# RWKV-7 layer of a hybrid trunk: triangular 32x32 blocks inverted by doubling on TensorE instead of a lane solve on VectorE

## The chip, the cores and the metric

The program runs on one core of a Trainium2 chip. The metric is the device time of one execution in microseconds (us); a comparison rests on the median of several. Engines are named as the profile names them: PE is TensorE's matmul stream, PEld its weight loads, DVE is VectorE, ACT is ScalarE, POOL is GpSimd, SP is the engine that issues the DMAs. Each engine takes its own instructions in a fixed order and waits at the first one whose inputs are not there.

## The reference, cut to what matters

The network has four layers over 256 context tokens and 1024 image tokens, width 1024: layers 0 and 3 are gated linear recurrences, layer 1 is an mLSTM, layer 2 is RWKV-7 with 16 heads of 64, run forwards and backwards. The change is in layer 2 alone, whose recurrence is

```
def step(s, inp):
    r_t, w_t, kk_t, a_t, k_t, v_t = inp
    s = (s * w_t[..., None, :]
         - jnp.einsum('bhvk,bhk->bhv', s, kk_t)[..., None] * (kk_t * a_t)[..., None, :]
         + v_t[..., :, None] * k_t[..., None, :])
    return s, jnp.einsum('bhvk,bhk->bhv', s, r_t)
```

All of it is in float32. The kernel works on chunks of 64 tokens. Within a chunk the rank-one corrections form a unit lower triangular 64x64 system, so each chunk of each head and direction needs the inverse of one such matrix.

## The kernel before, in words

Layer 2 is the function `rwkv_scan`. It first builds constants and projects the first token block, and then runs one loop of 41 rounds over 40 batches. A batch is one pair of heads, both directions, and one block of 256 tokens of each direction, which is four chunks per direction, so 2 heads x 2 directions x 4 chunks = 16 triangular matrices. Four things make up a round n, written in this order: the chunk steps `chain` of batches n-1 and n (four calls; the state goes from one step to the next), `finish` of batch n-2, `inverse` of batch n+1, and `prep` of batch n+2. Beside these each round pulls a portion of "fill": the projections of the other token blocks (products with 128x128 weights into the PSUM pool `pz`, lines 110 to 112 and 899 to 901), the gate and the output projection. The fill of a round may not be issued before the last DVE instruction of an earlier round. A scheduler then sets the final order on each engine from this code; it may put an instruction of one batch between those of another.

`prep` (lines 991 to 1111) makes, among other things, the tile DG: the two 32x32 diagonal blocks of each matrix. The 128 partitions are 4 groups of 32 rows (2 heads x 2 diagonal blocks), and u = 0 to 7 runs over direction and chunk. The 32x32 block below the diagonal goes to the tile OF.

`inverse` (lines 1113 to 1182) has three parts. The lane solve: DVE transposes DG (line 1122, on a tile of 1024 columns of which a quarter is used), so that each lane holds a whole 32x32 matrix in its row (tile LN); then 14 steps of forward substitution on the two 16x16 diagonal blocks of each, two DVE instructions a step (lines 1139 and 1140); then DVE transposes back (line 1142, tile DF). One doubling from 16 to 32: POOL masks DG to the 16x16 block below the diagonal (tile DO), DVE masks and adds the identity (D16) and transposes it (E16, line 1146); PE multiplies 32 blocks of 32x32 (line 1152), ACT copies the result out of PSUM (QQ, line 1154), PE multiplies again (line 1157), DVE adds (line 1159) and transposes (line 1160). The last doubling, from 32 to 64, uses OF, 16 products twice (lines 1164 and 1170) and ACT copies into the tile DT, which `chain` reads at line 1215. The products of one doubling use one PSUM tile of the pool `pi`, which has one buffer and is also used by `kk_norm` in the fill (lines 957 and 965).

The constants `m16`, `off16` and `id32` are built before the loop by POOL selects through the helper `sel` (line 787).

Of the kernel before, what the change touches and what calls it, by code (L numbers as in the profile page):

```python
# [28 lines left out]
class Net:  # L29
# [731 lines left out]
    def rwkv_scan(self, es, hd, zd, yd, xd):  # L761
        nc = self.nc
        gate = self.mod["gate"]
        V, G, S = nc.vector, nc.gpsimd, nc.scalar
        mm = nc.tensor.matmul
        rp = es.enter_context(self.pool("rp", 2))
        one = es.enter_context(self.pool("r1", 1))
        psp = lambda n, b: es.enter_context(self.tc.tile_pool(name=n, bufs=b, space=PSUM))
        pz, px, pc, pi = psp("pz", 2), psp("px", 2), psp("pc", 3), psp("pi", 1)
        tile_ = lambda name, shape, dt=F32, bufs=2: rp.tile(shape, dt, tag=name, name=name, bufs=bufs)  # L770
# [10 lines left out]
        def cst(name, shape, fill=0.0):  # L781
            t = one.tile(shape, F32, name=name)
            G.memset(t, fill)
            return t

        def sel(t, pattern, base, cm, op=ALU.is_ge, fill=0.0):
            G.affine_select(out=t, in_=t, pattern=pattern, compare_op=op, fill=fill, base=base, channel_multiplier=cm)
# [14 lines left out]
                        in1=hm.unsqueeze(1).to_broadcast([128, 8, 2]), op=ALU.mult)  # L802
# [188 lines left out]
        def prep(n):  # L991
# [10 lines left out]
                V.tensor_copy(out=w2[d][r], in_=raw2[r])  # L1002
                self.lo(G, w2[d][hr[1 - d]], raw2[r], w2[d][r])
            lw = L[i]
            DG = DGs[n % len(DGs)]
            b["DG"], b["OF"] = DG, tile_("OF", [128, 8, 32])
            ts, ops = [], []
            for d in (0, 1):
                blk = order[d][i]
# [103 lines left out]
        def inverse(n):  # L1113

            i, e = batch(n)
            b = B[n]
            DG, OF, DT = b["DG"], b["OF"], DTs[n % 2]
            u8 = lambda t: t.unsqueeze(1).to_broadcast([128, 8, 32])
            l8 = lambda name, tag=None: rp.tile([128, 8, 32], F32, tag=tag or name, name=name, bufs=1)
            DO = l8("DO")  # L1120
            LN = tile_("LN", [128, 32, 32], bufs=1)
            V.transpose(out=LN, in_=DG.rearrange("p u t -> p t u"))
            self.tt(G, DO, DG[:, 0:8, :], u8(off16))
            full = LN.rearrange("p t s -> p (t s)")

            def ap(t0, tn, s0, sn, tb, sb):

                v = full[:, t0 * 32 + s0:t0 * 32 + s0 + 1]
                dims = [list(v.ap[0]), [16 * 33, 2], [0 if tb else 32, tn], [0 if sb else 1, sn]]
                return bass.AP(v.tensor, v.offset, dims)  # L1130

            for j in range(1, 15):
                n1 = 15 - j
                tmp = tile_("ltmp", [128, 2, 56], bufs=1)
                c = ap(j + 1, n1, j, j, False, True)
                x = ap(j, n1, 0, j, True, False)
                o = ap(j + 1, n1, 0, j, False, False)
                tv = tmp[:, :, 0:n1 * j].rearrange("p q (t s) -> p q t s", s=j)
                V.tensor_tensor(out=tv, in0=c, in1=x, op=ALU.mult)
                V.tensor_tensor(out=o, in0=tv, in1=o, op=ALU.add)  # L1140
            DF = tile_("DF", [128, 32, 32], bufs=1)
            V.transpose(out=DF.rearrange("p u t -> p t u"), in_=LN)
            D16, E16 = l8("D16"), l8("E16", "E")
            self.tt(V, D16, DF[:, 0:8, :], u8(m16))
            self.tt(V, D16, D16, u8(id32), ALU.add)
            V.transpose(out=E16, in_=D16)
            p8 = lambda: pi.tile([128, 8, 64], F32, tag="pi", name="pi")
            ps = p8()
            g4 = [slice(32 * g, 32 * g + 32) for g in range(4)]
            for u in range(8):  # L1150
                for g in g4:
                    mm(ps[g, u, 0:32], DO[g, u, :], E16[g, u, :], start=True, stop=True)
            QQ = l8("QQ", "Q8")
            S.copy(out=QQ, in_=ps[:, :, 0:32])
            for u in range(8):
                for g in g4:
                    mm(ps[g, u, 32:64], QQ[g, u, :], D16[g, u, :], start=True, stop=True)
            D32, E32 = l8("D32"), l8("E32", "E")
            V.tensor_tensor(out=D32, in0=D16, in1=ps[:, :, 32:64], op=ALU.add)
            V.transpose(out=E32, in_=D32)  # L1160
            ps = p8()
            for u in range(8):
                for hh in (0, 2):
# [120 lines left out]
                    return  # L1284

        early = True
        h0 = [tile_(t, [128, 4, 256], bufs=1) for t in ("LN", "DF")]
        for k in range(8):
            nc.sync.dma_start(out=h0[k // 4][:, k % 4, :], in_=hd[k][:, 0:256])
        for _ in group((0,), (4, 5, 1, 0, 2)):  # L1290
# [9 lines left out]
        for r in hr:  # L1300
# [3 lines left out]
            sel(mk[1][r, 0:64], [[1, 64]], -64, 1)  # L1304
            sel(mk[1][r, 64:128], [[-1, 64]], 0, 1)
            sel(mb[1][r], [[-1, 64]], 63, -1)
        m16, off16, id32 = cst("m16", [128, 32], 1.0), cst("off16", [128, 32], 1.0), cst("id32", [128, 32], 0.0)
        for g in range(4):
            r = slice(32 * g, 32 * g + 32)
            V.tensor_copy(out=id32[r], in_=self.ident[r, r])  # L1310
            sel(m16[r], [[1, 32]], -1, -1)

            sel(off16[r, :], [[0, 32]], 15, -1)
        V.memset(off16[:, 0:16], 0.0)
        V.tensor_tensor(out=m16, in0=m16, in1=off16, op=ALU.subtract)
        scm = []
        for d in (0, 1):
            t = cst(f"scm{d}", [128, 4, 65], 1.0)
            V.memset(t[:, :, 64 - 64 * d:65 - 64 * d], 0.0)
            scm.append(t)  # L1320
        sgs = [cst(f"sg{d}", [128, 4, 65]) for d in (0, 1)]
        DGs = [cst(f"DG{i}", [128, 32, 32]) for i in range(1)]
        DTs = [cst(f"DT{i}", [128, 8, 64]) for i in range(2)]
        st = [[one.tile([128, 64], F32, name=f"st{e}{d}") for d in (0, 1)] for e in range(4)]
        G0, G1, G2 = (0,), (1, 4), (2, 3)
# [157 lines left out]
```

## Time and profile before

| | |
|---|---|
| median of 3 runs (lowest, highest) | 4810.22 us (4805.49, 4817.24) |
| the profiled execution's own time | 4812.02 us |
| its span in the trace | 4810.3 us |
| mean granted TensorE clock in it | 0.849 of full speed |
| busy share of the span: PE, PEld, DVE, ACT, POOL | 85%, 69%, 73%, 44%, 48% |

The loop over the 40 batches lies between about 2080 and 4180 us. "Busy" is the time in which at least one instruction of an engine runs; PE's instructions overlap, and their ends are modelled by the profiler. The granted clock of a stretch is the mean of two levels, 1.2 and 2.4 GHz; 0.75 means that half of the stretch ran at each.

### The profile page before, as it was taken

To read this page: it belongs to the slowest core of one execution; us is meant where nothing else is said; L and a number is where in the kernel's file an instruction comes from. 1 tells how busy PE (TensorE), PEld (TensorE's weight loads), DVE (VectorE), ACT (ScalarE), POOL (GpSimd) and SP (SyncE) were. 2 spreads that over 40 slices of the span, in tenths; PEclk is the share of its full clock that TensorE was granted. 3 is DMA by queue.
4 is the path that set the end of the run, shared out by engine and by line. 5 is a ranking of instruction groups with operands and counts; after the bars stand their busy time and mean duration, and the time that the engine had idled before them with its cause. 6 is when DMAs were issued, how large, how long until landed. Compare 5 with 4: busy or idle time off the path is not lost. (4 is left out here: it accounts for less than half of the span.)

```text
span 4810.3 us, 84381 instructions
## 1 busy us (share of the span) xinstructions
PE 4103.1 (85%) x31940; PEld 3342.1 (69%) x31940; DVE 3495.0 (73%) x6520; ACT 2101.5 (44%) x4458; POOL 2304.7 (48%) x1995
## 2 busy tenths in 40 slices
PE   5887898999999989668888888779788897669988
PEld 5676686888888878545667666566666676557766
DVE  6988846555555542696888879988898899657884
ACT  3555513222222210555656545445555444247661
POOL 4566623333333331375556545445456554247662
PEclk9898898999999989768788867567688787679999
DMA  4222331222222242434444433223334453231123
GB/s 158 85 73 76 139 107 47 90 88 90 97 91 90 88 156 66 151 119 130 131 133 140 126 98 114 83 83 105 91 123 134 142 166 103 82 110 51 50 85 104
DMA packets 322360, 504.53 MB, mean 105 GB/s; under 512 B 55680, under 2 KB 202112, under 8 KB 321824
## 3 DMA queue, kind: packets, MB, share of 16 engines
q1 hardware_dynamic: 321952, 499.12, 32.1%
q8 instruction: 252, 4.13, 0.3%
q14 instruction: 156, 1.28, 0.1%
HBM read 406.02 MB, written 92.96 MB: 104 GB/s over the span
## 5 line engine op out<-in xcount | busy, mean ns | idle before, releaser
L86 POOL TENSOR_TENSOR wlo<-wraw,whi 128x512 fp32r<-128x512 f32 (+3 forms) x437 | 727.6, 1666 | 986.1 <-DVE whi L101 441.7
L110 PE MATMUL pm<-hhi,whi 128*128 128x512 f32 (+1 forms) x1648 | 624.2, 379 | 48.7 <-DVE whi L101 47.7
L112 PE MATMUL pm<-hhi,wlo 128*128 128x512 f32 (+1 forms) x1648 | 616.6, 377 | 41.4 <-POOL wlo L86 41.3
L111 PE MATMUL pm<-hlo,whi 128*128 128x512 f32 (+1 forms) x1648 | 623.7, 379 | 10.1 <-DVE hlo L81 10.1
L110 PE MATMUL pz<-xh,whi 128*128 128x512 f32 (+1 forms) x784 | 341.5, 438 | 67.1 <-ACT xh L856 20.9
L110 PEld LDWEIGHTS pm<-hhi,whi 128*128 128x128 f32 x1648 | 319.5, 194 | 102.8 <-issue 28.0
L112 PEld LDWEIGHTS pm<-hhi,wlo 128*128 128x128 f32 x1648 | 317.9, 193 | 102.7 <-POOL wlo L86 51.9
L86 POOL TENSOR_TENSOR xl<-mx,xh 128x512 fp32r<-128x512 f32 (+1 forms) x240 | 282.9, 1182 | 218.1 <-ACT xh L856 182.0
L111 PEld LDWEIGHTS pm<-hlo,whi 128*128 128x128 f32 x1648 | 319.6, 194 | 64.7 <-DVE hlo L81 11.5
L101 DVE CAST whi<-wraw 128x1024 fp32r<-128x1024 f32 (+4 forms) x189 | 153.2, 810 | 277.3 <-PE pm L622 145.9
L111 PE MATMUL pz<-xl,whi 128*128 128x512 f32 (+1 forms) x784 | 334.9, 428 | 21.9 <-POOL xl L86 21.3
L110 PE MATMUL pm<-yhi,whi 128*128 128x512 f32 (+1 forms) x816 | 306.4, 380 | 45.4 <-DVE x L81 13.5
L112 PE MATMUL pz<-xh,wlo 128*128 128x512 f32 (+1 forms) x784 | 333.3, 426 | 4.2 <-POOL wlo L86 2.2
L111 PE MATMUL pm<-ylo,whi 128*128 128x512 f32 (+1 forms) x816 | 306.4, 376 | 3.5 <-POOL ylo L86 2.2
L112 PE MATMUL pm<-yhi,wlo 128*128 128x512 f32 (+1 forms) x816 | 299.5, 374 | 2.9 <-POOL wlo L86 2.9
L81 DVE SCALAR_TENSOR_TENSOR x<-pm,mod,x 128x512 f32<-128x512 f32 (+1 forms) x208 | 136.9, 665 | 188.4 <-PE pm L112 175.8
L110 PEld LDWEIGHTS pz<-xh,whi 128*128 128x128 f32 x784 | 178.8, 229 | 112.6 <-ACT xh L856 31.7
L1068 PE MATMUL px<-AR,BK 64*128 64x128 f32 x1280 | 197.8, 365 | 67.7 <-ACT BK L1046 24.2
L865 ACT CAST whi<-wraw 128x512 fp32r<-128x512 f32 x276 | 169.8, 617 | 158.6 <-PE pz L111 74.8
L81 DVE SCALAR_TENSOR_TENSOR mx<-hp,vecs,mx 128x256 f32<-128x256 f32 (+3 forms) x280 | 191.4, 706 | 60.0 <-ACT mx L836 59.0
L1068 PEld LDWEIGHTS px<-AR,BK 64*128 64x128 f32 x1280 | 167.4, 256 | 92.5 <-ACT BK L1046 35.5
L1140 DVE TENSOR_TENSOR LN<-ltmp,LN 128x28 f32<-128x28 f32 (+6 forms) x560 | 222.0, 396 | 12.3
(354 smaller groups left out, 11277.0 us busy)
## 6 DMA issues: line engine op xcount, KB each, us to landing
mw<-in_mod_w SPq DMA_DIRECT2D x160, 256.0 KB, 2.6
wraw<-in_r_w SPq DMA_DIRECT2D x144, 256.0 KB, 2.9
kin<-r7krk SPq DMA_DIRECT2D x72, 384.0 KB, 3.3
wraw<-in_lru_w_in SPq DMA_DIRECT2D x40, 512.0 KB, 3.6
hp<-r7h SPq DMA_DIRECT2D x160, 128.0 KB, 2.2
wraw<-in_r_wv SPq DMA_DIRECT2D x80, 256.0 KB, 2.9
UZ<-r7v SPq DMA_DIRECT2D x160, 128.0 KB, 2.9
hp<-r7h SPq DMA_DIRECT2D x120, 160.0 KB, 2.3
```

The costliest lines, as they stand in the source:

```text
L81: i = eng.scalar_tensor_tensor(out=out, in0=in0, scalar=scalar, in1=in1, op0=op0, op1=op1, **k)
L86: eng.tensor_tensor(out=out, in0=a, in1=b, op=op)
L101: nc.vector.tensor_copy(out=hi, in_=raw)
L110: mm(out, w[0][:, c], x[0][:, a:a + b], start=first, stop=False)
L111: mm(out, w[0][:, c], x[1][:, a:a + b], start=False, stop=False)
L112: mm(out, w[1][:, c], x[0][:, a:a + b], start=False, stop=last)
L865: S.copy(out=hi, in_=raw)
L1068: mm(pss[hh][:, c * 128:(c + 1) * 128], BK[r, c, 64 - 64 * hh:192 - 64 * hh], AR[r, c, :], start=True, stop=True)
L1140: V.tensor_tensor(out=o, in0=tv, in1=o, op=ALU.add)
```

## The change

The lane solve goes. POOL masks DG with the first of five constant masks, which keeps the entry below the diagonal of each 2x2 block; DVE adds the identity and transposes. Then come four equal doublings, from 2, 4, 8 and 16, each in the way the one from 16 was done: a POOL mask, 32 products, an ACT copy, 32 products, a DVE add and a DVE transpose. The last doubling, with OF, stays. DG shrinks to 256 columns and gets two buffers, as do the other tiles of `inverse`; the tiles that held the first block's activations get names of their own. The masks `lev` are built by 40 POOL selects where `m16` and `off16` took 8.

```diff
-            DO = l8("DO")
-            LN = tile_("LN", [128, 32, 32], bufs=1)
-            V.transpose(out=LN, in_=DG.rearrange("p u t -> p t u"))
-            self.tt(G, DO, DG[:, 0:8, :], u8(off16))
...
-            for j in range(1, 15):
...
-                V.tensor_tensor(out=tv, in0=c, in1=x, op=ALU.mult)
-                V.tensor_tensor(out=o, in0=tv, in1=o, op=ALU.add)
-            DF = tile_("DF", [128, 32, 32], bufs=1)
-            V.transpose(out=DF.rearrange("p u t -> p t u"), in_=LN)
-            D16, E16 = l8("D16"), l8("E16", "E")
-            self.tt(V, D16, DF[:, 0:8, :], u8(m16))
-            self.tt(V, D16, D16, u8(id32), ALU.add)
-            V.transpose(out=E16, in_=D16)
...
+            O = l8("O")
+            self.tt(G, O, DG, u8(lev[0]))
+            D32, E32 = l8("D"), l8("E")
+            self.tt(V, D32, O, u8(id32), ALU.add)
             V.transpose(out=E32, in_=D32)
+            for m in lev[1:]:
+                O = l8("O")
+                self.tt(G, O, DG, u8(m))
+                ps = p8()
+                for u in range(8):
+                    for g in g4:
+                        mm(ps[g, u, 0:32], O[g, u, :], E32[g, u, :], start=True, stop=True)
+                QQ = l8("QQ", "Q8")
+                S.copy(out=QQ, in_=ps[:, :, 0:32])
+                for u in range(8):
+                    for g in g4:
+                        mm(ps[g, u, 32:64], QQ[g, u, :], D32[g, u, :], start=True, stop=True)
+                D, E32 = l8("D"), l8("E")
+                V.tensor_tensor(out=D, in0=D32, in1=ps[:, :, 32:64], op=ALU.add)
+                V.transpose(out=E32, in_=D)
+                D32 = D
...
+        lev = [cst(f"lev{size}", [128, 32], 0.0) for size in (1, 2, 4, 8, 16)]
...
+            for m, size in zip(lev, (1, 2, 4, 8, 16)):
...
+                sel(v, [[-2 * size, nb], [0, size]], 0, 1)
+                sel(v, [[2 * size, nb], [0, size]], size - 1, -1)
...
-        DGs = [cst(f"DG{i}", [128, 32, 32]) for i in range(1)]
```

How the instructions stand, DVE, kernel before, one batch in the middle of the loop: the lane solve begins (LN is the transposed tile, ltmp its scratch), with an update of the state (UZ) of another batch and a mask of `prep` (X) between.

```order
L1122 STREAM_TRANSPOSE LN<-DG_16674 128x1024
L1077 TENSOR_TENSOR X_29111<-px,mk_16626 64x4x128
L1139 TENSOR_TENSOR ltmp<-LN 128x2x14
L1140 TENSOR_TENSOR LN<-ltmp,LN 128x2x14
L1139 TENSOR_TENSOR ltmp<-LN 128x2x26
L1140 TENSOR_TENSOR LN<-ltmp,LN 128x2x13x2
L1139 TENSOR_TENSOR ltmp<-LN 128x2x36
L81 SCALAR_TENSOR_TENSOR UZ<-UZ,W_27845,pc 64x64 x2
L81 SCALAR_TENSOR_TENSOR UZ<-UZ,W_27878,pc 64x64 x2
L1140 TENSOR_TENSOR LN<-ltmp,LN 128x2x12x3
```

All rows of lines 1122, 1139 and 1140 here are taken out by the change.

DVE, changed kernel, also in the middle of the loop: the ends of the last three doublings of one batch (D is the inverse so far, E its transpose) and the start of the next batch, with state updates (UZ, st) between.

```order
L1141 TENSOR_TENSOR D<-D,pi 128x256
L1142 STREAM_TRANSPOSE E<-D 128x256
L81 SCALAR_TENSOR_TENSOR UZ<-UZ,W_24728,pc 64x64 x2
L81 SCALAR_TENSOR_TENSOR UZ<-UZ,W_24761,pc 64x64 x2
L1141 TENSOR_TENSOR D<-D,pi 128x256
L1142 STREAM_TRANSPOSE E<-D 128x256
L1141 TENSOR_TENSOR D<-D,pi 128x256
L1142 STREAM_TRANSPOSE E<-D 128x256
L86 TENSOR_TENSOR D<-O,id_16644 128x256
L81 SCALAR_TENSOR_TENSOR st_16721<-UZ,W_24728,pc 64x64 x2
L81 SCALAR_TENSOR_TENSOR st_16722<-UZ,W_24761,pc 64x64 x2
L1127 STREAM_TRANSPOSE E<-D 128x256
```

The 28 lane steps and both wide transposes are gone from DVE; a pair of add and transpose stands there once for each doubling.

PE, kernel before, the second half of one batch's inverse: lines 1157, 1164 and 1170 are products of `inverse`, the others belong to `finish`, `prep` (lines 1018 and 1020) and the fill.

```order
L1273 MATMUL px<-ident,y 64x64 x11
L1106 MATMUL px<-rkb,tp 128x2 x2
L1157 MATMUL pi<-D_27696,QQ 32x32 x32
L1018 MATMUL px<-lhi_27234,w_28449 128x256 x2
L1020 MATMUL px<-llo,w_28449 128x256 x2
L1018 MATMUL px<-lhi_27235,w_28450 128x256 x2
L1020 MATMUL px<-llo,w_28450 128x256 x2
L110 MATMUL pz<-xh,whi 128x512
L1164 MATMUL pi<-E_27769,OF 32x32 x16
L111 MATMUL pz<-xl,whi 128x512
L112 MATMUL pz<-xh,wlo 128x512
L1170 MATMUL pi<-D_27768,QP 32x32 x16
```

Between two sets of products of the inverse stood other products here.

PE, changed kernel, the end of one batch's inverse in a round with much fill: lines 1134 and 1139 are the two products of a doubling, 1147 and 1153 those of the last one; the others are steps of `chain`.

```order
L1198 MATMUL pc<-U_34268,DT_16717 64x64 x4
L1134 MATMUL pi<-E,O 32x32 x32
L1211 MATMUL pc<-UZ,X_32443 64x64 x2
L1211 MATMUL pc<-UZ,X_32476 64x64 x2
L1213 MATMUL pc<-UZ,RB_32479 64x64 x2
L1213 MATMUL pc<-UZ,RB_32501 64x64 x2
L1139 MATMUL pi<-D,Q_33829 32x32 x32
L1134 MATMUL pi<-E,O 32x32 x32
L1139 MATMUL pi<-D,Q_33902 32x32 x32
L1147 MATMUL pi<-E,OF 32x32 x16
L1153 MATMUL pi<-D,Q_33957 32x32 x16
```

Where four sets of products stood in PE's order for a batch, ten stand now; here the last five follow each other with nothing between.

## Rows read from the trace of the kernel before

**Rows 1.** The page's first part: busy time, share of the span, instructions.

```profile
PE 4103.1 (85%) x31940; PEld 3342.1 (69%) x31940; DVE 3495.0 (73%) x6520; ACT 2101.5 (44%) x4458; POOL 2304.7 (48%) x1995
```

**Rows 2.** Windows: length, busy us of PE, PEld, DVE, ACT, POOL, clock, DMA.

```profile
2080.00:4180.00 2100.00, 1743.97 (x19606) 1341.77 (x19603) 1797.70 (x3729) 1078.25 (x2808) 1137.16 (x1199) 0.75 0.38 117
1800.00:1900.00 100.00, 100.00 (x516) 84.60 (x515) 25.49 (x37) 5.10 (x4) 19.87 (x10) 1.00 0.21 60
2400.00:2600.00 200.00, 174.34 (x1858) 132.11 (x1859) 167.33 (x316) 117.93 (x296) 120.29 (x121) 0.82 0.45 137
3000.00:3200.00 200.00, 154.80 (x1723) 118.38 (x1724) 180.74 (x377) 90.00 (x238) 100.31 (x111) 0.64 0.30 94
3400.00:3600.00 200.00, 160.94 (x1853) 126.45 (x1854) 180.35 (x385) 111.78 (x297) 105.11 (x114) 0.70 0.35 110
3800.00:4000.00 200.00, 169.43 (x2056) 135.74 (x2052) 182.60 (x379) 87.43 (x244) 115.36 (x124) 0.86 0.53 163
```

**Rows 3.** Windows again: three short stretches of the loop.

```profile
2710.00:2755.00 45.00, 43.70 (x610) 33.75 (x608) 28.41 (x55) 27.43 (x76) 20.67 (x21) 0.99 0.39 123
2761.00:2836.00 75.00, 64.81 (x568) 51.32 (x568) 70.45 (x161) 34.85 (x99) 36.48 (x44) 0.50 0.31 94
3007.00:3096.00 89.00, 64.70 (x802) 51.95 (x802) 80.91 (x180) 41.42 (x110) 41.34 (x50) 0.50 0.25 76
```

**Rows 4.** DVE groups in the loop: count | busy, mean ns | idle before, releaser.

```profile
L1140 DVE TENSOR_TENSOR LN<-ltmp,LN 128x28 f32<-128x28 f32 (+6 forms) x560 | 222.0, 396 | 12.3
L1139 DVE TENSOR_TENSOR ltmp<-LN 128x28 f32<-128x28 f32 (+6 forms) x560 | 218.8, 391 | 12.1
L1122 DVE STREAM_TRANSPOSE LN<-DG 128x1024 f32<-128x1024 f32 x40 | 79.9, 1997 | 12.5 <-ACT DG L1074 12.0
L1142 DVE STREAM_TRANSPOSE DF<-LN 128x1024 f32<-128x1024 f32 x40 | 79.7, 1992 | 0.9
...
L86 DVE TENSOR_TENSOR D<-DF,m 128x256 f32<-128x256 f32 x40 | 24.0, 600 | 0.6
L86 DVE TENSOR_TENSOR D<-D,id 128x256 f32<-128x256 f32 x40 | 22.7, 568 | 0.6
L1146 DVE STREAM_TRANSPOSE E<-D 128x256 f32<-128x256 f32 x40 | 17.5, 436 | 4.2 <-PE pi L1164 3.6
...
L1159 DVE TENSOR_TENSOR D<-D,pi 128x256 f32<-128x256 f32 x40 | 16.6, 414 | 11.5 <-PE pi L1157 10.8
```

**Rows 5.** Groups in the loop: products of the inverse and their weight loads.

```profile
L1152 PE MATMUL pi<-E,DO 32*32 32x32 f32 x2560 | 42.6, 215 | 18.0 <-DVE kq L81 9.5 <-DVE E L1146 8.5
L1157 PE MATMUL pi<-D,QQ 32*32 32x32 f32 x2560 | 40.8, 214 | 2.4 <-ACT QQ L1154 2.3
...
L1152 PEld LDWEIGHTS pi<-E,DO 32*32 32x32 f32 x2560 | 34.6, 126 | 29.8 <-DVE kq L81 10.9 <-DVE E L1146 8.3 <-issue 3.2
L1164 PE MATMUL pi<-E,OF 32*32 32x32 f32 x1280 | 34.3, 211 | 30.2 <-DVE E L1160 24.7 <-DVE ltmp L1139 2.8 <-DVE s L1264 2.7
L1157 PEld LDWEIGHTS pi<-D,QQ 32*32 32x32 f32 x2560 | 33.6, 126 | 13.3 <-issue 5.7 <-ACT QQ L1154 3.0 <-ACT mx L836 0.7
```

**Rows 6.** Timeline of PE, two places: start, duration of one set of 32 products.

```profile
3931.00 0.75 PE L1152 MATMUL pi<-E,DO 32*32 32x32 f32 x64
...
2796.03 1.07 PE L1152 MATMUL pi<-E,DO 32*32 32x32 f32 x64 [0.16 <-DVE E L1146]
```

**Rows 7.** Groups in the loop: the POOL mask and the ACT copy of a doubling.

```profile
L86 POOL TENSOR_TENSOR DO<-DG,off 128x256 f32<-128x256 f32 x39 | 31.5, 807 | 34.1 <-ACT DG L1074 25.1 <-PE pi L1152 8.9
...
L1154 ACT COPY QQ<-pi 128x256 f32<-128x256 f32 x40 | 14.8, 370 | 19.6 <-PE pi L1152 19.2
```

**Rows 8.** The selects of line 787: duration ns min/median/max, first and last start.

```profile
L787 POOL TENSOR_SCALAR_AFFINE_SELECT m<-m x4: 205/260/426, 1972.5 to 1974.1; 32x32 f32<-32x32 f32 x4
```

**Rows 9.** Waits in the loop: total us, times, longest us.

```profile
PEld pi L1152 <- DVE kq L81: 10.9, 6, 3.1
```

More of the change, by code (lines that the diff above doesn't have):

```diff
@@ L1004, in prep @@
             lw = L[i]
-            DG = DGs[n % len(DGs)]
-            b["DG"], b["OF"] = DG, tile_("OF", [128, 8, 32])
+            DG = b["DG"] = tile_("DG", [128, 8, 32])
+            b["OF"] = tile_("OF", [128, 8, 32])
             ts, ops = [], []
@@ L1118, in inverse @@
             u8 = lambda t: t.unsqueeze(1).to_broadcast([128, 8, 32])
-            l8 = lambda name, tag=None: rp.tile([128, 8, 32], F32, tag=tag or name, name=name, bufs=1)
-            DO = l8("DO")
-            LN = tile_("LN", [128, 32, 32], bufs=1)
-            V.transpose(out=LN, in_=DG.rearrange("p u t -> p t u"))
-            self.tt(G, DO, DG[:, 0:8, :], u8(off16))
[L1124 to L1130, printed above, removed]
@@ L1132, in inverse @@
-            for j in range(1, 15):
[L1133 to L1138, printed above, removed]
-                V.tensor_tensor(out=tv, in0=c, in1=x, op=ALU.mult)
-                V.tensor_tensor(out=o, in0=tv, in1=o, op=ALU.add)
-            DF = tile_("DF", [128, 32, 32], bufs=1)
@@ L1142, in inverse @@
-            V.transpose(out=DF.rearrange("p u t -> p t u"), in_=LN)
-            D16, E16 = l8("D16"), l8("E16", "E")
-            self.tt(V, D16, DF[:, 0:8, :], u8(m16))
-            self.tt(V, D16, D16, u8(id32), ALU.add)
-            V.transpose(out=E16, in_=D16)
+            l8 = lambda name, tag=None: tile_(tag or name, [128, 8, 32])
             p8 = lambda: pi.tile([128, 8, 64], F32, tag="pi", name="pi")
-            ps = p8()
             g4 = [slice(32 * g, 32 * g + 32) for g in range(4)]
-            for u in range(8):
-                for g in g4:
-                    mm(ps[g, u, 0:32], DO[g, u, :], E16[g, u, :], start=True, stop=True)
@@ L1153, in inverse @@
[L1153 to L1159, printed above, removed]
-            V.transpose(out=E32, in_=D32)
+            O = l8("O")
+            self.tt(G, O, DG, u8(lev[0]))
+            D32, E32 = l8("D"), l8("E")
@@ L1286, in rwkv_scan @@
         early = True
-        h0 = [tile_(t, [128, 4, 256], bufs=1) for t in ("LN", "DF")]
+        h0 = [tile_(t, [128, 4, 256], bufs=3) for t in ("X0", "X1")]
         for k in range(8):
@@ L1306, in rwkv_scan @@
             sel(mb[1][r], [[-1, 64]], 63, -1)
-        m16, off16, id32 = cst("m16", [128, 32], 1.0), cst("off16", [128, 32], 1.0), cst("id32", [128, 32], 0.0)
+        id32 = cst("id32", [128, 32], 0.0)
+        lev = [cst(f"lev{size}", [128, 32], 0.0) for size in (1, 2, 4, 8, 16)]
         for g in range(4):
@@ L1310, in rwkv_scan @@
             V.tensor_copy(out=id32[r], in_=self.ident[r, r])
[L1311 to L1315, printed above, removed]
+            for m, size in zip(lev, (1, 2, 4, 8, 16)):
+                v = m[r].rearrange("p (b x) -> p b x", x=2 * size)[:, :, size:]
+                nb = 16 // size
+                if g == 0:
+                    G.memset(m.rearrange("p (b x) -> p b x", x=2 * size)[:, :, size:], 1.0)
+                sel(v, [[-2 * size, nb], [0, size]], 0, 1)
+                sel(v, [[2 * size, nb], [0, size]], size - 1, -1)
         scm = []
```

## The prediction

> **What bounds the kernel now.** The page's first part comes first: over the whole program PE is busy 85% and DVE 73% [rows 1], so neither is alone the limit. That is a mean over four layers, so the windows come next, for the loop that the change is in, 2080 to 4180 us: 2100 us, DVE busy 1798 us (86%), PE 1744 (83%), POOL 1137 (54%), ACT 1078 (51%) [rows 2]. Two engines stand close to full, and they take turns. From 3000 to 3200 DVE is at 90% and PE at 77%; the same picture holds from 3400 to 3600 [rows 2]. In the short stretches it is sharper: 3007 to 3096 has DVE at 91% and PE at 73%, while 2710 to 2755 has DVE at 63% and PE at 97% [rows 3]. The reader should also look at the clock column. The two stretches in which DVE is above 90% ran at a granted clock of 0.50, all of it at 1.2 GHz; the one with DVE at 63% ran at 0.99 [rows 3]. The mean is 0.75, half of the loop at each level [rows 2]. So a DVE that is late costs twice: PE waits, and what PE then does, it does at the lower clock. Of everything on DVE the lane solve is the largest single thing: 560 + 560 small instructions and 80 wide transposes, 600 us of 1798 [rows 4].
>
> **What leaves DVE.** Per batch: the two wide transposes, 1.997 + 1.992 = 3.99 us; 14 steps of two instructions, 14 x (0.391 + 0.396) = 11.02 us; the mask to 16x16 blocks, 0.60 us. Together 15.61 us. The addition of the identity (0.568) and the first small transpose (0.436) stay, and the one doubling that was there stays [rows 4]. Three doublings are added, each an addition out of PSUM and a transpose, 0.414 + 0.436 = 0.85 us, so 2.55 us. The net is 13.06 us a batch, 522 us over 40 batches. DVE's busy time in the loop goes from 1798 to 1276 us, 61% of today's 2100. This is certain as work and says nothing yet about time.
>
> **What PE gets.** Three more doublings of two sets of 32 products. One set took 0.75 us in a place at full clock and 1.07 us in one at half clock [rows 6]; over the loop the groups give 42.6/40 = 1.07 and 40.8/40 = 1.02 us [rows 5]. Three times two sets are 4.5 us a batch if all ran at full clock, 6.3 us by the means, so 180 to 250 us over the loop. I take 250, since the mean contains the places where a set is cut in two by other products. PE's busy time at today's clock is then 1744 + 250 = 1994 us, 95% of 2100.
>
> **What ACT and POOL get.** ACT has three more copies of 0.370 us, 44 us over the loop, and goes from 1078 to 1122 us; POOL has five masks of 0.807 us where it had one, 129 us, and goes from 1137 to 1266 us, 60% [rows 2, 7]. Both stay far from full, so I cost this work at nothing beside PE; what it costs if that cover is gone is its own size, 129 us at most. The masks do not depend on the doublings and can be made ahead. Nothing is added to the DMA queues.
>
> **New waits.** Each doubling hands over from PE to ACT, to PE, to DVE and back to PE. Four sets of products per batch become ten, and in the new order some follow each other directly with no other product between, so there PE's queue, with the state steps and the fill behind, stands until ACT or DVE has answered. Today's sets bound the price: PE was idle 18.0 us before the first set and 30.2 us before line 1164, but only 2.4 us before line 1157, over 40 batches each [rows 5], so 0.06 to 0.76 us a hand-over. Six more per batch are 14 to 182 us over the loop. These waits are not added to the sum below, they are what keeps PE's share below 100%. All doublings also share the one PSUM buffer with the normalisation in the fill; today that costs PE's weight loads 10.9 us [rows 9], and with five uses per batch instead of two it is 27 us if it grows with them, 0 if the order avoids it.
>
> **The start.** 40 selects replace 8. At 0.205 to 0.260 us each [rows 8] the 32 more take 7 to 8 us of POOL before the first projections; with the old wide buffer's clearing gone and some of it beside other work I take 4 us, between 0 and 8.
>
> **The sum.** DVE no longer ends last; PE does. Two things must be chosen, PE's share of the loop and its clock. For the share the nearest row is the stretch with DVE at 63%, where PE reached 97% [rows 3]; with the added hand-overs I take 95%. For the clock, DVE-bound stretches gave 0.50 and that light one 0.99 [rows 3]; in 200 us windows it was 0.64 and 0.70 where DVE was at 90%, and 0.82 where it was at 84%; 3800 to 4000, with 0.86 at a DVE share of 91%, shows that DVE's share alone does not set it [rows 2]. I take 0.82, so 36% of the loop at half clock in place of 50%. A set took 1.43 times as long at half clock [rows 6], so busy time goes as 1 + 0.43 x that part: from 1.215 to 1.155, a factor of 0.951. Then PE is busy 1994 x 0.951 = 1896 us, the loop lasts 1896/0.95 = 1996 us, 104 us less, and with 4 us at the start the profiled execution of 4812 us would take 4712. That execution lies 2 us above the median of the runs, which does not matter here. I forecast **4710 us**. Its own range is 4650 to 4790.
>
> **Rival 1: the whole relief arrives.** If the loop runs as it did from 3800 to 4000 in its clock, 0.86, and at the 97% of the light stretch [rows 2, 3], the factor is 1.120/1.215 = 0.922, PE is busy 1838 us and the loop takes 1895 us: 205 us less, 4611 us. For it speaks that PE's weight loads, which overlap products less, were busy only 1342 us in the loop, 64%, and reached 85% in a dense stretch of another layer [rows 2]. With three times 34.6 + 33.6 us added [rows 5] they are 1547 us; at 85% that is 1829 us and 4545 us for the kernel. Against it speaks that this dense stretch has long products without hand-overs. The Trainium skill, Perfetto Trace Analysis, section Identifying the Most-Contended Engine, states the rule behind this: the busy share of matmuls is a poor measure of TensorE's headroom, and that of the weight loads a good one. By that rule TensorE had a third of the loop free. The trace agrees so far that the one share is 83% and the other 64% in the same window [rows 2].
>
> **Rival 2: PE becomes the bound, and the kernel is slower.** If the clock stays at 0.75 and PE's share is 92%, the loop takes 1994/0.92 = 2167 us, 67 us more, about **4880 us**. The mechanism is PE's own queue: ten sets in fixed order, each waiting on ACT or DVE for the one before, with the state steps behind them, so that the time DVE gave back turns up as PE's idle time; that the stretches with small products and little fill ran at 0.50 [rows 3] speaks for it. It decides at a share of 92% when the granted clock stays below 0.79: above that, 1994 x (1 + 0.43 x 0.41)/1.215/0.92 falls under 2100. Against it speaks that the low clock stood where DVE held PE up. The Trainium skill, TensorE: Matmul & The Clock Gate, section A second HAM failure mode: psum-queue depth-cycling, tells of a kernel in which short idle times between groups of products, as PSUM banks were cycled, made the clock swing between its levels and lowered throughput. By that rule the ten sets through one buffer would push the clock down: at the 0.70 of 3400 to 3600 [rows 2] the sum gives 1994 x 1.258/1.215/0.92 = 2244 us and 4960 us. No row here shows the clock around such a series.
>
> **Rival 3: nothing moves.** PE at today's clock and a share of 95% gives 1994/0.95 = 2099 us, the time of today. What DVE gave up then returns exactly as PE's work.
>
> **How the numbers follow.** The forecast gets 0.46, rival 1 0.20, rival 2 0.22 and rival 3 0.12. A change of 0.3%, about 14 us, is what a measurement of this kernel can tell from none. Faster by more is the forecast and rival 1, 0.66; the same 0.12; slower 0.22. The range of 8 in 10 leaves out the outer half of rivals 1 and 2: 4570 to 4880 us.
>
> **What would show it.** DVE's busy time in the loop near 1280 us and no wide transposes in its groups; the products of the doublings near 6 to 8 us a batch more on PE; PE's share of the loop near 95%, with a granted clock above 0.80. If the granted clock stays at 0.75 or falls, the forecast is wrong in that step and rival 2 or 3 holds. If PE's share stays at 83% although DVE is at 61%, then neither engine was the bound but the hand-overs between them, and the row to look at is PE's idle time before the sets of a doubling. If POOL's waits grow by more than its 129 us, the cover I gave it was not there.

## The result and the profile after

The changed kernel takes 5006.24 us (4996.77 to 5018.70), the kernel before 4813.73 us (4805.49 to 4823.13), each the median of four runs: a ratio of 1.040, 95% interval 1.037 to 1.043. It is slower by 193 us where 100 us less were forecast; rival 2, the slower case, stood at 4880.

The page of the changed kernel, first part (busy us, share of the span, instructions), and its instruction queue (packets, MB, share of the DMA engines):

```profile
PE 4321.1 (86%) x47300; PEld 3559.4 (71%) x47300; DVE 3080.7 (62%) x5518; ACT 2142.9 (43%) x4578; POOL 2425.3 (48%) x2194
...
q8 instruction: 371, 6.08, 0.5%
```

Against [rows 1] PE has 218 us more and DVE 414 us less, so the work moved as the change says. All of the time is in the loop. Here it is from 2080 us to the last state step, first before and then after (length, busy us of PE, PEld, DVE, ACT, POOL, granted clock, DMA share, GB/s); what follows it takes 619 us in both.

```profile
2080.00:4192.00 2112.00, 1753.12 (x19721) 1349.22 (x19718) 1802.82 (x3742) 1080.51 (x2815) 1139.84 (x1201) 0.75 0.38 117
```

```profile
2080.00:4385.00 2305.00, 1976.79 (x35119) 1569.41 (x35117) 1391.12 (x2746) 1126.80 (x2946) 1260.79 (x1367) 0.73 0.36 108
```

DVE went from 85% of the loop to 60%, and yet PE stands idle nearly as long: 2112 - 1753 = 359 us before, 2305 - 1977 = 328 us after. The clock did not rise but fell a little. The groups of the inverse after (line, engine, operation and tiles, count | busy us, mean ns | idle before it and its releasers) answer to [rows 4, 5, 7]. The profile counts each of these products twice, so 10240 is 160 sets of 32:

```profile
L1139 PE MATMUL pi<-D,Q 32*32 32x32 f32 x10240 | 158.5, 212 | 25.7 <-ACT Q L1136 20.0 <-issue 4.9
L1134 PE MATMUL pi<-E,O 32*32 32x32 f32 x10240 | 155.9, 215 | 28.0 <-DVE E L1142 26.6 <-DVE kq L81 1.3
...
L1153 PE MATMUL pi<-D,Q 32*32 32x32 f32 x1280 | 35.5, 216 | 13.1 <-ACT Q L1150 13.1
L1147 PE MATMUL pi<-E,OF 32*32 32x32 f32 x1280 | 32.2, 205 | 21.7 <-DVE E L1142 21.4 <-issue 0.4
...
L1142 DVE STREAM_TRANSPOSE E<-D 128x256 f32<-128x256 f32 x160 | 70.6, 441 | 3.7
L1141 DVE TENSOR_TENSOR D<-D,pi 128x256 f32<-128x256 f32 x160 | 67.0, 419 | 199.7 <-PE pi L1139 187.9 <-ACT whi L865 9.1 <-ACT xh L937 0.8
...
L1136 ACT COPY Q<-pi 128x256 f32<-128x256 f32 x160 | 59.1, 369 | 95.7 <-PE pi L1134 93.8
...
L86 POOL TENSOR_TENSOR O<-DG,lev 128x256 f32<-128x256 f32 x200 | 161.3, 807 | 178.2 <-PE pi L1134 132.1 <-DVE D L86 40.2 <-ACT DG L1074 2.3
```

A set of an ordinary doubling costs 155.9/160 = 0.97 us and 158.5/160 = 0.99 us; an addition 0.419, a transpose 0.441, a copy 0.369, a mask 0.807 us, all as before. The right-hand side is what is new. DVE, which stood 10.8 us before the 40 additions of a doubling [rows 4], now stands 187.9 us before 160, and POOL 132.1 us before masks that wait for a buffer. What stands behind such a wait in the engine's order comes later; how much of this idle time PE then had to wait for is not shown.

One batch's doublings, seen from PE: its timeline (start us, us, line, tiles, count, and in brackets the idle time before and its releaser), and the window over the same stretch.

```profile
2929.89 0.75 PE L1134 MATMUL pi<-E,O 32*32 32x32 f32 x64
2931.30 0.45 PE L1211 MATMUL pc<-UZ,X 128*64 128x64 f32 x8 [0.65 <-DVE st L81]
2931.68 0.53 PE L1213 MATMUL pc<-UZ,RB 64*64 64x64 f32 x8
2932.13 1.06 PE L1139 MATMUL pi<-D,Q 32*32 32x32 f32 x61
2933.53 0.31 PE L1139 MATMUL pi<-D,Q 32*32 32x32 f32 x3 [0.33 <-issue]
2934.99 1.08 PE L1134 MATMUL pi<-E,O 32*32 32x32 f32 x64 [1.16 <-DVE E L1142]
2936.61 1.06 PE L1139 MATMUL pi<-D,Q 32*32 32x32 f32 x61 [0.54 <-ACT Q L1136]
2938.98 0.31 PE L1139 MATMUL pi<-D,Q 32*32 32x32 f32 x3 [1.31 <-issue]
2940.45 1.06 PE L1147 MATMUL pi<-E,OF 32*32 32x32 f32 x32 [1.15 <-DVE E L1142]
2942.39 0.80 PE L1153 MATMUL pi<-D,Q 32*32 32x32 f32 x22 [0.88 <-ACT Q L1150]
```

```profile
2929.00:2943.00 14.00, 7.47 (x334) 6.37 (x336) 6.30 (x15) 4.40 (x14) 6.72 (x10) 0.60 0.39 116
```

From 2933 on nothing but sets of the inverse stands in PE's order, each behind an answer from ACT or DVE. PE is busy 7.5 of 14 us, and a set that took 0.75 us at 2929.89 takes 1.06 us at 2932.13, the two lengths of [rows 6]: the clock went to its lower level here.

This stretch is near the extreme, and it is not what most rounds look like. Taken over the 40 batches of the changed kernel, the stretches from the first to the last of a batch's last six sets have PE busy 83% of the time and a granted clock of 0.80, above the 0.73 of the loop; in only one of them is PE idle for a larger share than here. In this one, of another round, other products stand between the sets:

```profile
3212.00:3227.00 15.00, 13.41 (x409) 10.91 (x409) 7.70 (x19) 9.13 (x26) 8.20 (x9) 1.00 0.28 90
```

### The profile page after: what moved, and what is told of

Same layout as the page of the kernel before. It is cut to its first block, busy times and chain, and to the rows that moved or that the text cites. A ratio compares the mean times of both kernels' runs of the same rounds, so it can differ in the third digit from the quotient of the medians.

```text
span 5003.6 us, 114594 instructions
## 1 busy us (share of the span) xinstructions
PE 4321.1 (86%) x47300; PEld 3559.4 (71%) x47300; DVE 3080.7 (62%) x5518; ACT 2142.9 (43%) x4578; POOL 2425.3 (48%) x2194
## 3 DMA queue, kind: packets, MB, share of 16 engines
q8 instruction: 371, 6.08, 0.5%
## 5 line engine op out<-in xcount | busy, mean ns | idle before, releaser
L110 PE MATMUL pz<-xh,whi 128*128 128x512 f32 (+1 forms) x784 | 330.1, 423 | 66.3 <-ACT xh L856 27.0
L112 PE MATMUL pz<-xh,wlo 128*128 128x512 f32 (+1 forms) x784 | 320.5, 409 | 7.2 <-POOL wlo L86 5.1
L81 DVE SCALAR_TENSOR_TENSOR mx<-hp,vecs,mx 128x256 f32<-128x256 f32 (+3 forms) x280 | 213.4, 787 | 164.7 <-ACT mx L836 163.8
L1068 PE MATMUL px<-AR,BK 64*128 64x128 f32 x1280 | 219.1, 380 | 46.0 <-DVE X L1077 32.4
L86 POOL TENSOR_TENSOR O<-DG,lev 128x256 f32<-128x256 f32 x200 | 161.3, 807 | 178.2 <-PE pi L1134 132.1
L1068 PEld LDWEIGHTS px<-AR,BK 64*128 64x128 f32 x1280 | 184.7, 269 | 67.8 <-DVE X L1077 38.1
```

The costliest lines, as they stand in the source:

```text
L81: i = eng.scalar_tensor_tensor(out=out, in0=in0, scalar=scalar, in1=in1, op0=op0, op1=op1, **k)
L86: eng.tensor_tensor(out=out, in0=a, in1=b, op=op)
L110: mm(out, w[0][:, c], x[0][:, a:a + b], start=first, stop=False)
L112: mm(out, w[1][:, c], x[0][:, a:a + b], start=False, stop=last)
L1068: mm(pss[hh][:, c * 128:(c + 1) * 128], BK[r, c, 64 - 64 * hh:192 - 64 * hh], AR[r, c, :], start=True, stop=True)
```

## The experiments

Each run is compared with runs of the kernel before on the same chip (medians 4802 to 4811 us there). Four questions were asked: was VectorE a bound at all; what do the hand-overs of the added doublings cost and what their products; do the buffers and the masks matter; and is a point between the two kernels better. All loop figures go from 2080 us to the last state step.

### Relief without the price: x_none and b_half

x_none leaves the three added doublings out, so that PE has the four sets of before and DVE no lane solve; the tile that held the inverse is kept at zero.

```diff
-            for m in lev[1:]:
+            for m in lev[4:]:
...
+        G.memset(lev[0], 0.0)
+        V.memset(id32, 0.0)
```

> The changed kernel without the three added doublings at all (masks, products, copies, additions, transposes left out); the first mask and the identity are zero. PE has the same work as in the kernel before, DVE some 620 us less in the loop. If DVE was a bound of the kernel before, as my prediction had it, the time is 4700 us or below, and 4600 if it was the main one. If PE's order of work alone set the pace, it lies within 30 us of 4812.

Measured: 4572.49 us, ratio 0.951 (0.948 to 0.954), below the 4600 that were to mean that DVE was the main bound.

b_half is the kernel before with seven of its 14 lane steps left out.

```diff
-            for j in range(1, 15):
+            for j in range(1, 8):
```

> The kernel before with 7 of the 14 steps of the lane solve left out, so DVE has 14 small instructions a batch less, about 5.5 us, 220 us over the loop; nothing else changes. If DVE was a bound, the time falls by 80 to 200 us, to 4610 to 4730. If DVE's busy share did not matter, it stays between 4790 and 4815.

Measured: 4667.08 us, ratio 0.970 (0.968 to 0.972), as expected if DVE was a bound. The loops, x_none and then b_half:

```profile
2080.00:3946.00 1866.00, 1652.68 (x19752) 1276.35 (x19750) 1298.39 (x2505) 1074.73 (x2828) 1189.69 (x1248) 0.82 0.43 133
```

```profile
2080.00:4047.00 1967.00, 1690.15 (x19712) 1311.42 (x19710) 1621.41 (x3179) 1070.33 (x2813) 1139.17 (x1198) 0.78 0.41 125
```

VectorE was a bound. The first 181 us taken from it (1803 to 1621) shorten the loop by 145, 0.8 us for each; the 504 us of x_none shorten it by 246, so the further 323 us give 101, 0.3 for each. With PE's work unchanged the clock rises from 0.75 to 0.78 and 0.82. The last figure is the one that the prediction took, and PE's busy time, 1653 us, is what it would have worked out for this case: 1744 x 0.951 = 1659. But PE's share is 1653/1866 = 89%, not 95%.

### The price in two parts: x_few and x_free

x_few is the changed kernel with the added doublings' sets cut from 32 products to 4, every copy, addition, transpose, mask and wait kept; the copy and the addition read the four results for all eight blocks, so what comes out is not the inverse.

```diff
+                nu = 8 if m is lev[4] else 1
...
-                for u in range(8):
+                for u in range(nu):
...
-                S.copy(out=QQ, in_=ps[:, :, 0:32])
+                S.copy(out=QQ, in_=ps[:, :, 0:32] if nu == 8 else ps[:, 0:1, 0:32].to_broadcast([128, 8, 32]))
```

> The changed kernel, but in the three added doublings (from 2, 4 and 8) each set has 4 products in place of 32; the ACT copy, the DVE addition and the transpose keep their sizes and their waits. It leaves out seven eighths of those products. PE loses about 6 x 0.85 us a batch, some 175 to 200 us over the loop; all hand-overs stay. If the hand-overs between PE, ACT and DVE are what made the change slower, the time stays at 4950 us or above. If PE's time for the products is, it falls by 150 to 200 us, to 4800 to 4850 us.

Measured: 4777.07 us, ratio 0.993 (0.990 to 0.996).

x_free is the opposite: all products and masks of the added doublings stay, but nothing is copied, added, transposed or waited for between them.

```diff
+                if m is not lev[4]:
+                    for u in range(8):
+                        for g in g4:
+                            mm(ps[g, u, 32:64], O[g, u, :], D32[g, u, :], start=True, stop=True)
+                    continue
```

> The changed kernel, but the products of the three added doublings read tiles that are ready after the first step and nothing reads their results: all products and masks stay, the three copies, additions and transposes and all their waits go. The first mask and the identity are set to zero, so the inverse is zero. If the hand-overs are the cause, the time falls to 4830 us or below. If PE's time for the products is, it stays at 4960 us or above.

Measured: 4921.16 us, ratio 1.023 (1.020 to 1.025). The loops, x_few and then x_free:

```profile
2080.00:4166.00 2086.00, 1811.51 (x21672) 1396.83 (x21671) 1386.28 (x2745) 1121.99 (x2949) 1261.72 (x1368) 0.74 0.39 119
```

```profile
2080.00:4327.00 2247.00, 1888.02 (x35120) 1491.66 (x35120) 1310.30 (x2507) 1082.39 (x2827) 1263.74 (x1367) 0.77 0.36 111
```

Both runs miss their expectations. x_few lies below the 4800 to 4850 us that were to mean that the products are the price, x_free between its two branches. Taken out alone, most of the added products are worth 229 us, more than the whole loss; the copies, additions, transposes and waits, taken out alone, are worth 85 (66 against x_zero, below, which has the same zeros). Put on top of x_none the other way round, everything but most of the products costs 205 us, and the products with the masks 349. So the split depends on the order in which the parts are added.

In the order x_none, x_few, changed kernel the loop says where the time goes. The step to x_few adds 220 us: PE is busy 159 us longer and idle 61 us longer. By the ratio of [rows 6] the fall of the clock from 0.82 to 0.74 makes 1653 us into 1653 x 1.224/1.155 = 1751, so by this estimate about 99 us of the 159 are clock and 60 are the few products. The step to the changed kernel adds 219 us: PE is busy 165 us longer (some 12 of it clock) and idle 54 us longer. Together, from x_none to the changed kernel: products about 213 us, clock about 111, idle time 115, 439 in all, against 246 that the lane solve gave back. That is the 193. The groups of the doublings bear out the products: 100 us in x_none, 145 in x_few and 314 in the changed kernel. Their lines in x_none and then in x_few:

```profile
L1134 PE MATMUL pi<-E,O 32*32 32x32 f32 x2560 | 55.6, 205 | 8.7 <-DVE kq L81 6.7 <-DVE E L1127 1.9
L1139 PE MATMUL pi<-D,Q 32*32 32x32 f32 x2560 | 44.1, 205 | 1.5 <-ACT Q L1136 1.5
```

```profile
L1135 PE MATMUL pi<-E,O 32*32 32x32 f32 x3520 | 72.6, 218 | 35.7 <-DVE E L1143 31.9 <-POOL UZ L1194 2.7 <-POOL tp L86 1.0
L1140 PE MATMUL pi<-D,Q 32*32 32x32 f32 x3520 | 72.0, 215 | 10.8 <-ACT Q L1137 10.5
```

Two things are not separated in the 205 us. They hold the work of the added doublings on the other engines beside the waits: DVE is busy 88 us longer in x_few than in x_none, and x_mask below puts the three masks at up to 58 us. And that the waits are what lowered the clock is not shown: the clock is lower in the runs that have them, but within the changed kernel it is not lower where the last sets of a batch stand (0.80) than in the loop as a whole (0.73).

x_free costs more than x_few although nothing waits there for an answer: 349 us above x_none (its profiled execution is 27 us longer than its median). Some of it is a cost that the changed kernel hardly has, which b_sets shows.

### Products on the kernel before: b_sets

```diff
+            for _ in range(3):
+                for u in range(8):
+                    for g in g4:
+                        mm(ps[g, u, 0:32], DO[g, u, :], E16[g, u, :], start=True, stop=True)
+                for u in range(8):
+                    for g in g4:
+                        mm(ps[g, u, 32:64], DO[g, u, :], D16[g, u, :], start=True, stop=True)
```

> The kernel before with six more sets of 32 products a batch, ahead of its own doubling, which read tiles that are ready and hand nothing over (their result is overwritten): the disputed 250 us of products by themselves, with VectorE as full as it was. Theory (products cost loop time one to one or more, as the 349 us between the runs without hand-overs and without the doublings say, because TensorE's idle time comes in short waits that they cannot fill): 5000 to 5150 us. Rival A (they fall into the 356 us in which TensorE stands idle behind VectorE): 4820 to 4900. Rival B (half and half): 4900 to 5000.

Measured: 5076.78 us, ratio 1.057 (1.055 to 1.060). The loop, and the groups of the added sets and their own doubling's first set:

```profile
2080.00:4457.00 2377.00, 1909.12 (x35103) 1511.11 (x35102) 1793.10 (x3741) 1085.58 (x2821) 1138.63 (x1205) 0.75 0.34 105
```

```profile
L1156 PE MATMUL pi<-D,DO 32*32 32x32 f32 x7680 | 144.2, 221 | 55.1 <-issue 55.1
L1153 PE MATMUL pi<-E,DO 32*32 32x32 f32 x7680 | 144.1, 218 | 57.8 <-issue 30.9 <-DVE E L1146 23.6 <-DVE kq L81 1.9
L1159 PE MATMUL pi<-E,DO 32*32 32x32 f32 x2560 | 45.7, 228 | 23.7 <-issue 23.7
```

The theory holds in its sum, 265 us more loop for 240 sets, 1.1 us a set, and none of it fell into PE's idle time behind DVE. But its parts are two: 156 us more busy time, and 55 + 31 + 24 = 110 us in which PE stood with the next product not there ("issue"). In the changed kernel the same groups show 5 us of that. So by PE's busy time the products are worth about 156 us here, less than the 213 estimated above. That the rest of b_sets and 90 us of x_free belong to seven sets standing in a row is the likely reading.

### Zeros: x_zero

In x_none, x_free and x_mask the inverse's tiles hold zeros. x_zero is the changed kernel with those two lines alone (lev[0] and id32 cleared).

> The changed kernel with the constants lev0 and id32 zero and nothing else altered, as they are in the runs without doublings, without hand-overs and with two masks; the inverses are then zero, and the result is not the reference's. It tells how much of those runs' gains comes from the zeros. Theory (an engine's time here does not depend on the numbers): 4985 to 5030 us, so 4572, 4921 and 4929 us in those runs are due to what they left out. Rival (products of zeros let the clock stand higher): 4880 to 4960 us, and those gains would have to be read against this run.

Measured: 4987.05 us, ratio 1.038 (1.036 to 1.040), against 1.040 of the changed kernel, as the theory had it: zeros explain some 10 to 20 us of those runs.

### Buffers and masks: x_pi2, b_pi2, x_obuf, x_pi2_obuf, x_mask

x_pi2 gives the doublings a second PSUM buffer, at the cost of one of the chain's three; b_pi2 does the same to the kernel before.

```diff
-        pz, px, pc, pi = psp("pz", 2), psp("px", 2), psp("pc", 3), psp("pi", 1)
+        pz, px, pc, pi = psp("pz", 2), psp("px", 2), psp("pc", 2), psp("pi", 2)
```

> The changed kernel with two PSUM buffers for the products of the doublings and two in place of three for the chain's. Theory (sets and hand-overs): the doublings of one batch are a chain in themselves, so a second buffer gives nothing, and one chain buffer less costs 0 to 1%: 4990 to 5060 us. Rival (the one buffer, held some 27 us a batch, keeps TensorE from the next batch's doublings): 4880 to 4950.

> The kernel before with two PSUM buffers for the inverse's products and two in place of three for the chain's. Theory (the buffer is short only where ten sets use it): no change, 4790 to 4830 us. Rival (the second buffer, or the order that follows from it, helps any kernel with this loop): 4710 to 4750, and the 93 us in the changed kernel would then say nothing about the change.

Measured: x_pi2 4913.13 us, ratio 1.021 (1.018 to 1.025); b_pi2 4760.28 us, ratio 0.991 (0.989 to 0.993). The changed kernel's loop with two buffers, and the wait that answers to DVE's 187.9 us above:

```profile
2080.00:4282.00 2202.00, 1894.18 (x35108) 1486.86 (x35106) 1413.87 (x2741) 1124.41 (x2945) 1266.57 (x1367) 0.77 0.37 113
```

```profile
DVE D L1141 <- PE pi L1139: 116.1, 54, 8.7
```

The theory that a second buffer gives nothing, because one batch's doublings are a chain, fell: 93 us, as the rival had it. The same buffer also serves the normalisation in the fill, which may be the reason. But b_pi2 lies between its two expectations: the kernel before, with four sets, gains 42 us too, so about half of the 93 is not owed to the change. Fewer buffers also change the order that the scheduler makes, and these runs don't separate the two.

x_obuf gives each of the five masked tiles a buffer of its own and masks all ahead of the first product; x_pi2_obuf has both.

```diff
-            O = l8("O")
-            self.tt(G, O, DG, u8(lev[0]))
+            Os = [tile_(f"O{k}", [128, 8, 32]) for k in range(5)]
+            for O, m in zip(Os, lev):
+                self.tt(G, O, DG, u8(m))
+            O = Os[0]
```

> The changed kernel with a buffer for each of the five masked tiles O0 to O4, all masked ahead of the first product; GpSimd then no longer waits within the doublings (its 132 us of waiting for the sets that read O). Theory (the sets and their hand-overs through ScalarE and VectorE are the price): 4980 to 5020 us, no change. Rival (GpSimd's queue held behind the masks delays its other work and through it the chain): 4870 to 4940.

> The changed kernel with both: two PSUM buffers for the doublings and a buffer for each masked tile. If the two are different causes their gains add up: 4913 - 30 = 4870 to 4895 us. If they are one cause (the doublings' sets held in a row by whichever buffer is short): 4900 to 4920. In either case it stays slower than before, since products and hand-overs remain.

Measured: x_obuf 4978.71 us, ratio 1.035 (1.031 to 1.038); x_pi2_obuf 4872.35 us, ratio 1.014 (1.012 to 1.016). x_obuf ends a little below its theory's range and far from the rival's; x_pi2_obuf lies where two separate causes were to put it. POOL's wait for buffers is worth about 27 us alone and 41 on top of x_pi2: a cause of its own, and a small one. With both repaired the changed kernel is still slower than before.

x_mask keeps only the first and last of the five masks; the doublings between read the first one's tile.

```diff
-                O = l8("O")
-                self.tt(G, O, DG, u8(m))
+                if m is lev[4]:
+                    O = l8("O")
+                    self.tt(G, O, DG, u8(m))
```

> The changed kernel with two of the five GpSimd masks kept, and the doublings between reading the first one's tile (the constants lev0 and id32 are zero, so numbers are small; the result is not the reference's). GpSimd loses 120 masks of 0.81 us, 97 us. Theory (sets and hand-overs on TensorE are the price, GpSimd has room): 4960 to 5000 us. Rival (GpSimd's masks stretch VectorE's operations beside them and hold up the chain): 4860 to 4920.

Measured: 4929.40 us, ratio 1.024 (1.021 to 1.027), between the two expectations; 58 us below x_zero, which has the same zeros. Three masks a batch are 120 x 0.807 = 97 us of POOL. By x_obuf some 27 to 41 us of the 58 may be the wait for their buffers; the rest can't be told apart from the new order.

### Between the two: lane8 and lane8_pi2

lane8 stops the lane solve at 8x8 blocks, six steps on four blocks in place of 14 on two, and follows it with two doublings. lane8_pi2 is lane8 with the PSUM buffers of x_pi2. Neither leaves anything of the computation out.

```diff
-                dims = [list(v.ap[0]), [16 * 33, 2], [0 if tb else 32, tn], [0 if sb else 1, sn]]
+                dims = [list(v.ap[0]), [8 * 33, 4], [0 if tb else 32, tn], [0 if sb else 1, sn]]
...
-            for j in range(1, 15):
-                n1 = 15 - j
-                tmp = tile_("ltmp", [128, 2, 56], bufs=1)
+            for j in range(1, 7):
+                n1 = 7 - j
+                tmp = tile_("ltmp", [128, 4, 12], bufs=1)
...
+            for O, k in ((DO, 0), (DO2, 1)):
```

> The midpoint between the two kernels: the lane solve on VectorE stops at 8x8 blocks (6 steps on four blocks in place of 14 on two), and two doublings follow in place of one (before) or five (after). Theory (VectorE was a bound of the loop and gives about 0.7 us for each us taken from it; an added doubling costs the same each time, (205 + 229) / 3 = 145 us by the runs without products and with few): some 16 of 28 lane operations go, about -215 us net of VectorE, so -150, and one doubling +145: 4805 us, within 1% of before. Rival A (the doublings after the first find no cover, the first finds it, in the 450 us that TensorE stands idle): the added one costs under 60 us, 4700 to 4730. Rival B (lane operations are fixed costs, shorter ones save little): 4880 or more.

> The midpoint (lane solve to 8x8 blocks, two doublings) with two PSUM buffers for the doublings and two in place of three for the chain. Theory (the one buffer costs in proportion to the sets that pass through it beyond the four of before: 93 us for six more, so 31 us for two more): 4700 to 4730 us. Rival (with two doublings the buffer is free in time, and one chain buffer less costs): 4745 to 4790.

Measured: lane8 4748.10 us, ratio 0.987 (0.985 to 0.990); lane8_pi2 4715.94 us, ratio 0.981 (0.978 to 0.984). The loops, lane8 and then lane8_pi2:

```profile
2080.00:4123.00 2043.00, 1771.63 (x24834) 1374.23 (x24836) 1605.22 (x3175) 1087.12 (x2853) 1179.88 (x1242) 0.78 0.40 121
```

```profile
2080.00:4103.00 2023.00, 1741.19 (x24838) 1354.37 (x24838) 1623.55 (x3171) 1086.88 (x2853) 1177.56 (x1242) 0.78 0.40 122
```

The midpoint beats both kernels. DVE loses 198 us of busy time in lane8, and by the 0.8 of b_half that is worth 158 us of loop; 69 came, so the one doubling added cost about 90 us, where each of the three in the changed kernel cost (205 + 229)/3 = 145. That lies between the theory's 145 and rival A's "under 60"; the 4748 us are above A's own range of 4700 to 4730. (The 450 us of idle TensorE that A names are 359 in the loop before.) The second PSUM buffer gives 25 us here when each run is set against its own runs of the kernel before, and 32 by the two medians (the theory's 31); it gives 42 us in the kernel before, so this is no support for the theory's rule that its worth grows with the sets.

## Why the prediction was wrong, point by point

**What bounds the kernel, and what leaves DVE: right in kind.** DVE did hold PE up, and less of it raised the clock to the 0.82 that was taken, as x_none shows. DVE's busy time fell by 412 us in the loop, not 522. The inverse's own operations came as forecast (517 us less); operations that the change doesn't touch took some 105 us more in sum, though not each of them (`AR<-kin,EN` fell from 741 to 606 ns). One that grew, before and after:

```profile
L81 DVE SCALAR_TENSOR_TENSOR AR<-kin,vecs,EN 128x256 f32<-128x256 f32 x78 | 52.8, 676 | 0.2
```

```profile
L81 DVE SCALAR_TENSOR_TENSOR AR<-kin,vecs,EN 128x256 f32<-128x256 f32 x78 | 60.8, 780 | 2.5 <-ACT EN L1035 1.1 <-POOL tp L86 0.8
```

**What PE gets: near, and on the high side.** 250 us of products were forecast at the old clock; the runs give about 213 by the estimate above and 156 in b_sets.

**The sum: here it failed, in both chosen numbers.** The step that failed is that PE would run nearly without gaps once DVE had room, at 95% and a clock of 0.82; the added doublings took both away. PE's share of 95% was measured as 1977/2305 = 86%. It came from one stretch of 45 us at 97% [rows 3], and no loop of 40 batches here held it: x_none, with no added hand-over and DVE at 70%, reaches 89%, and no other run here more. With 86% the sum's own 1896 us of PE give 1896/0.858 = 2210 us of loop in place of 1996, so 214 us of the miss. The clock of 0.82 was measured as 0.73: by the sum's formula PE's 1994 us are then 1994 x 1.232/1.215 = 2022, and the loop 2022/0.858 = 2357, 147 us more. PE's work was 45 us less than that, 52 us of loop. 214 + 147 - 52 = 309, the distance from 1996 to 2305. Of these 12 us are only the later end of the window (2112 us before in place of 2100); the rest, 297, is the miss of 296 us in the whole.

**New waits: the mechanism was named, and had no term of its own in the sum.** The 14 to 182 us of six more hand-overs were to be what keeps PE's share below 100%, in a share that the row of 45 us had already fixed. Measured, three doublings with 4 products a set cost 205 us, 220 in the profiled loops, and of these 61 as PE's idle time and about 99 as clock, with the other engines' work for these doublings in it. The price per wait, 0.06 to 0.76 us, holds the (26.6 + 20.0)/320 = 0.15 us measured as PE's own idle time; but a lower clock came with it, and DVE's 188 us and POOL's 132 us of waiting in order, which were not asked about. That the one PSUM buffer costs 0 to 27 us was too low: a second buffer gives 93 us, of which 42 also without the change.

**ACT and POOL at nothing: not so for POOL.** The masks were said to be makeable ahead; with two buffers for O, all but the first two wait for the sets of an earlier doubling. POOL's idle time before the masks grew from 34.1 us [rows 7] to 178.2, by more than 129 us, which the prediction named as the sign that the cover is not there. x_mask and x_obuf price it at 27 to 58 us, within the 129 us given as the cost in that case.

**The start** was of no weight: the first projection of the layer starts at 1975.61 us in place of 1974.84.

**The rivals.** Rival 2 names much of what happened: PE's queue of ten sets, each behind an answer, a clock below 0.79, part of the time of DVE returned as PE's waiting (115 of the 439 us; products and clock are the rest). Its 92% was still too high a share, so it too ended 126 us too low. The rule cited there, of the Trainium skill, TensorE: Matmul & The Clock Gate, section A second HAM failure mode: psum-queue depth-cycling, agrees with these traces in its direction from run to run: 0.82 in x_none, 0.74 with the hand-overs of x_few, and 0.77 instead of 0.73 with a second buffer. Within the changed kernel they do not bear it out: 0.60 in the 14 us shown above, but 0.80 over all the batches' last six sets, and in the kernel before a second buffer left the clock at 0.75 (b_pi2); why the clock fell stays open. Rival 1 rested on PE's weight loads being busy only 64%. After the change they are at 1569/2305 = 68%, and the loop is 193 us longer, although by that count a third of it is still free; in none of the loops here do they pass 69%. The rule cited there, of the Trainium skill, Perfetto Trace Analysis, section Identifying the Most-Contended Engine, gave no help in this loop: the weight loads' share showed time in which TensorE was free, not time that the loop could use.

What would have warned is in the text itself: PE's idle time before the sets of a doubling was named as the row to look at if PE's share stayed at 83%. [rows 5] already had 30.2 us before 40 sets of line 1164, which stand alone behind an answer as many of the ten do now. At 0.76 us for each of six, 182 us more would have made the sum 4710 + 182 = 4892, slower than before. That would have been the right direction by a wrong price: PE's idle time came to 0.15 us a set, and most of the loss came as products and clock.

## What to carry to other kernels

When work is moved from a busy engine to a chain of short steps that go from engine to engine, add the price of each hand-over to the sum, for every engine that waits in order, and ask which granted clock the new order will get; don't hide it in a busy share. Take a share that an engine can reach from the longest stretch that looks like the new loop, not from the best short one. Where the relief shrinks with each step taken (0.8, then 0.3 us per us here) and each added step costs about the same or more, look for a point between: solving to 8x8 blocks and doubling twice, with a second PSUM buffer, gives 4716 us where the two ends give 4814 and 5006.

## What the runs showed of the hardware

The changed program's instruction queue moved 371 packets and 6.08 MB. Before:

```profile
q8 instruction: 252, 4.13, 0.3%
```

That is 119 packets and 1.95 MB more, some 16 KB a packet, for 30,720 more PE instructions. Where seven sets stood in a row without a wait (b_sets, x_free), PE stood 110 and 90 us at "issue" for the next product; in the changed kernel, whose sets come one by one behind waits, it was 6 us. That the supply of instructions is what held PE there is inferred, not shown: all three programs moved the same 371 packets.

Why DVE operations that the change does not touch took 676 ns before and 780 ns after is open. In x_mask, with 90 us less on POOL, this one takes 706 ns, but others stay at their new length (779 against 791 ns for `ta<-ta,kin`), so POOL's masks are not the whole cause; and in b_sets, where DVE and POOL have the work of before, the first one already takes 742 ns.
